# A gated delta-rule encoder: the query product of the scan taken from plain rows, its decay applied on the way out of the bank

## The chip, the cores and the metric

The kernel runs on one core of a Trainium2 chip, as one launch. The metric is the time of that launch on the device in microseconds (us); lower is better. The engines are called PE (matmul; PEld is its weight load), DVE (vector), ACT (scalar), POOL (GpSimd) and SP (which only issues DMAs here). ACT issues some DMAs too.

## The reference

Two layers; each has a mixer and a SwiGLU feed-forward network on 1040 rows (16 meta tokens and 1024 inputs) of width 1024. In the mixer, four heads of width 128 run a chunked gated delta rule in both directions of time. What matters here is how one direction makes its outputs (cut):

```python
def chunk_gated_delta_rule(q, k, v, g, beta):
    G = jnp.cumsum(g, axis=-1)                       # log-decay, <= 0, per head and row
    decay_mat = jnp.exp(jnp.where(incl, G[..., :, None] - G[..., None, :], -jnp.inf))
    ...
    attn = jnp.einsum('bnhid,bnhjd->bnhij', q, k) * decay_mat
    q_dec = q * jnp.exp(G)[..., None]
    ...
    def step(S, inp):
        u_c, w_c, qd_c, kd_c, a_c, gl_c = inp
        v_new = u_c - jnp.einsum('bhcd,bhde->bhce', w_c, S)
        o = jnp.einsum('bhcd,bhde->bhce', qd_c, S) + jnp.einsum('bhij,bhje->bhie', a_c, v_new)
        S = S * gl_c[..., None, None] + jnp.einsum('bhcd,bhce->bhde', kd_c, v_new)
        return S, o

o = (o_fwd + o_bwd)[:, N_PAD:]
o = o * lax.rsqrt(jnp.mean(o * o, axis=-1, keepdims=True) + RMS_EPS)
o = (o * dn_norm_w.astype(jnp.float32) * jax.nn.silu(zf)).reshape(Bsz, L, DN_WIDTH)
```

The factor `exp(G)` is one number for each row and head, so it can be put on the query before the product with the state `S`, or on the product's rows.

## The kernel before, in words

Everything is float32. The dense projections (`dense`, L157 to L159) split weights and activations into a high and a low part and add three products in one bank of the matmul's accumulator memory. ACT makes the high part of a weight tile (`whi`, L130), POOL, or DVE at places, the low part (`wlo`, L131). The delta rule's own products are plain float32.

A chunk is 128 rows; the kernel has nine (chunk 0 is the 16 meta rows). For one layer the order is: projections of k, q, v and of the gates; the decay matrices (`chunk_p`); the inverse of each chunk's triangular matrix, direction 0 and then 1 (`substitute` and `invert`, of which L545, L546, L581 and L582 are transposes and copies on DVE and L561 to L596 small matmuls with copies on ACT); the attention matrices and scaled queries (`chunk_a`); the scan; the output projection; the feed-forward network.

`chunk_a(c)` makes on PE the products of keys and queries of chunk `c` (`qk`, L490) into a bank of tag `b`, of which there are two. For each of two directions `d` ACT's queue loads a broadcast of `exp(G)` (`eg<-ged`, L494) and the decay matrix (`dt<-dtd`, L499), DVE multiplies the query with the first (L495) and `qk` with the second (L500), and SP stores both to DRAM (`aqd`, L497 and L502). `eg` and `dt` come from one ring of five buffers (`t2k`, tag `ck2`), so a load waits until the store out of the buffer five tiles earlier has landed. A bank of `qk` comes free with the second L500 of its chunk. Between these pieces PE works on dense projections; `jobs`, `jobs2` and `jobs3` are lists of such pieces, of which one of each is put behind every dense block of columns.

`scan_step(d, c)` runs one chunk of one direction with the state `St[d]` and two banks, `b0` and `b1` (tag `f` for direction 0, `b` for direction 1). Per head: `ks = K S` into `b0` (L806); DVE makes `r` (L809); `vr = Z r` into `b1` (L812); ACT reads `vr` scaled (L816) and plain (L818); `su` into `b0` (L822); the output `po` into `b1`: first the scaled query times `S` (L835), then the attention matrix times `vn` (L836), in one accumulation group; DVE updates the state (L844). The first direction to reach a chunk copies `po` out on ACT (L849) and stores it (`od`, L850); the second calls `finalize`, which loads it again (L862), adds (L863), normalises with ACT and DVE, transposes on PE (L875) and multiplies with the gate rows `sz` (L860, L876) into `O`. `rec` has four slots of 128x512 for each direction; V, K, A and the scaled query fill them.

The program's order on each engine is set when it is built, by a scheduler that goes by the priorities in the code (`at_prio`) and by its own estimate of times. An engine runs its instructions in that order, and so does each DMA queue.

## Time and profile before

| | |
|---|---|
| median of 3 runs | 2581.15 us (2574.96 to 2581.61) |
| the profiled execution's own time | 2581.81 us |
| its span (first to last instruction) | 2580.0 us |
| PE busy | 2501.8 us, 97% of the span |
| DVE, ACT, POOL busy | 64%, 41%, 44% |
| mean DMA rate | 140 GB/s, 360.04 MB in all |
| `chunk_a` and the inverse's second half run in | 225 to 300 us and 1515 to 1592 us |
| the scan runs in | 336 to 540 us and 1638 to 1842 us |

The profile lists instructions by line, engine and form with their durations, and for each idle time of an engine what ended it. Matmuls are pipelined, so one that is shown with 0.32 us can follow the last after 0.16 us; the distance of their starts is their cost. An idle time counts only where the engine that idles is the one that all others wait for, which is PE here.

### The profile page before, as it was taken

What the parts mean: (1) busy time and instruction counts of PE and PEld (TensorE: products, weight loads), DVE (VectorE), ACT (ScalarE), POOL (GpSimd) and SP (SyncE); (2) the same over time, 40 slices, a digit from 0 to 9 for tenths busy, and PEclk for the clock granted to TensorE, in tenths of its full rate; (3) what the DMA queues carried; (4) which work ended last, traced back from release to release, by engine and by line L of the source; (5) the groups of instructions that cost most, each with busy time, mean ns of one, the idle gap of its engine ahead of it and who ended that gap; (6) DMA issues with size and microseconds to landing.
All of it is one profiled execution on the core that took longest, in us unless ns stands there. A gap on an engine that the chain in (4) does not pass through costs nothing. (4 is left out here: it accounts for less than half of the span.)

```text
span 2580.0 us, 45319 instructions
## 1 busy us (share of the span) xinstructions
PE 2501.8 (97%) x17508; PEld 2284.7 (89%) x17508; DVE 1660.6 (64%) x2461; ACT 1045.1 (41%) x1945; POOL 1138.4 (44%) x869
## 2 busy tenths in 40 slices
PE   8999999999999999999999998999998999999998
PEld 6989899998899999999998987999977778887787
DVE  4678423648766666678656884235597776768664
ACT  5664232435233333444445742224452333334444
POOL 2141212325666666655420312212466676675663
PEclk9999999999999999999999999999999999999999
DMA  3445665524432222574323556556343322228631
GB/s 127 137 154 171 210 190 165 195 75 130 136 109 87 88 82 81 193 233 140 96 92 122 173 169 209 171 166 204 106 135 115 117 90 94 87 88 268 188 119 70
DMA packets 213764, 360.04 MB, mean 140 GB/s; under 512 B 25460, under 2 KB 87868, under 8 KB 213548
## 3 DMA queue, kind: packets, MB, share of 16 engines
q1 hardware_dynamic: 180300, 310.17, 36.6%
q10 hardware_dynamic: 31072, 42.61, 5.3%
q0 software_dynamic: 2176, 4.36, 0.5%
q8 instruction: 137, 2.24, 0.4%
q14 instruction: 79, 0.65, 0.1%
HBM read 266.60 MB, written 90.46 MB: 138 GB/s over the span
## 5 line engine op out<-in xcount | busy, mean ns | idle before, releaser
L131 POOL TENSOR_TENSOR wlo<-raw,whi 128x512 fp32r<-128x512 f32 x132 | 176.8, 1341 | 760.1 <-ACT whi L130 666.3
L157 PE MATMUL pacc<-a,whi 128*128 128x346 f32 (+1 forms) x808 | 263.9, 330 | 8.8 <-ACT whi L130 6.5
L159 PE MATMUL pacc<-a,wlo 128*128 128x346 f32 (+1 forms) x808 | 264.8, 329 | 0.5 <-DVE wlo L131 0.3
L157 PE MATMUL pacc<-b,whi 128*128 128x346 f32 (+2 forms) x672 | 235.4, 351 | 0.1
L159 PE MATMUL pacc<-b,wlo 128*128 128x346 f32 (+2 forms) x672 | 233.2, 348 | 0.2 <-POOL wlo L131 0.2
L158 PE MATMUL pacc<-a,whi 128*128 128x346 f32 (+1 forms) x688 | 227.1, 330 | 0.6 <-DVE a L178 0.3
L130 ACT ACTIVATE whi<-raw 128x512 fp32r<-128x512 f32 x168 | 105.2, 628 | 277.3 <-PE pacc L158 158.6
L158 PE MATMUL pacc<-b,whi 128*128 128x346 f32 (+2 forms) x580 | 200.9, 347 | 0.3 <-DVE b L906 0.3
L1048 POOL TENSOR_TENSOR wlo<-rw,whi 128x512 fp32r<-128x512 f32 x92 | 134.7, 1466 | 71.8 <-ACT whi L1047 70.4
L157 PEld LDWEIGHTS pacc<-a,whi 128*128 128x128 f32 x808 | 153.4, 191 | 13.2 <-ACT whi L130 8.2
L159 PEld LDWEIGHTS pacc<-a,wlo 128*128 128x128 f32 x808 | 154.2, 191 | 2.1 <-POOL wlo L131 0.5
L157 PEld LDWEIGHTS pacc<-b,whi 128*128 128x128 f32 x672 | 127.1, 189 | 12.0 <-issue 3.1
L158 PEld LDWEIGHTS pacc<-a,whi 128*128 128x128 f32 x688 | 131.4, 191 | 5.2 <-issue 3.3
L1048 POOL TENSOR_TENSOR a<-rw,a 128x512 fp32r<-128x512 f32 x64 | 105.5, 1651 | 68.3 <-ACT a L1047 68.2
L159 PEld LDWEIGHTS pacc<-b,wlo 128*128 128x128 f32 x672 | 127.3, 190 | 9.4 <-issue 0.8
L1048 POOL TENSOR_TENSOR b<-rw,b 128x512 fp32r<-128x512 f32 x64 | 92.4, 1446 | 84.2 <-ACT b L1047 50.1
L158 PEld LDWEIGHTS pacc<-b,whi 128*128 128x128 f32 x580 | 109.8, 189 | 7.5 <-DVE b L906 0.6
L1047 ACT ACTIVATE whi<-rw 128x512 fp32r<-128x512 f32 x92 | 57.8, 630 | 144.4 <-DVE rw L1293 82.5
L1294 DVE TENSOR_TENSOR rw<-raw,rw 128x512 f32<-128x512 f32 x44 | 98.9, 2247 | 1.2
L1289 DVE TENSOR_TENSOR rw<-rw,rw 128x512 f32<-128x512 f32 x44 | 68.2, 1550 | 48.2 <-POOL wlo L1048 30.9
L1048 POOL TENSOR_TENSOR wlo<-raw,whi 128x512 fp32r<-128x512 f32 x50 | 79.0, 1583 | 32.5 <-ACT whi L1047 32.2
L1047 ACT ACTIVATE b<-rw 128x512 fp32r<-128x512 f32 x64 | 40.3, 630 | 122.3 <-PE pacc L1066 35.2
(970 smaller groups left out, 8439.3 us busy)
## 6 DMA issues: line engine op xcount, KB each, us to landing
raw<-in_w_in SPq DMA_DIRECT2D x112, 256.0 KB
raw<-in_w_gu SPq DMA_DIRECT2D x104, 256.0 KB
rw<-in_w_gu SPq DMA_DIRECT2D x88, 256.0 KB
rw<-in_w_dn SPq DMA_DIRECT2D x94, 192.0 KB
rec<-aqd SPq DMA_DIRECT2D x62, 256.0 KB
rec<-vkd SPq DMA_DIRECT2D x61, 256.0 KB
raw<-in_w_out SPq DMA_DIRECT2D x48, 256.0 KB
b<-ad SPq DMA_DIRECT2D x45, 260.0 KB
```

What stands on the lines that cost most here:

```text
L130: whi_done[0] = act(out=hi, in_=raw[:, 0:kk, :], func=AF.Copy)
L131: (tt if lov[0] else ptt)(out=lo, in0=raw[:, 0:kk, :], in1=hi.bitcast(F32), op=ALU.subtract)
L157: mm(ps[:, :n], wh, xh[:, n0:n1], start=(k == 0), stop=False)
L158: mm(ps[:, :n], wh, xl[:, n0:n1], start=False, stop=False)
L159: mm(ps[:, :n], wl, xh[:, n0:n1], start=False, stop=(k == K - 1))
L1047: act(out=hi, in_=src, func=AF.Copy)
L1048: ptt(out=lo, in0=src, in1=hi.bitcast(F32), op=ALU.subtract)
L1289: tt(out=s1t, in0=A21, in1=A22, op=ALU.add)
L1294: tt(out=A21, in0=A11, in1=A21, op=ALU.subtract)
```

## The change

The scaled queries are no longer made. `gates` drops the table `ged`; `chunk_a` drops `eg`, L495 and the store of the scaled query, and `aqd` has half its size. `scan_step` multiplies the plain query rows `QT`, which stay in their place on chip, with the state into `b1` ahead of `vr` (L802 of the changed kernel), and ACT copies each head out into a new tile `qs` with the scale `negE`, which is minus `exp(G)` (L804). `po` then holds the attention part alone. The first direction to reach a chunk subtracts `qs` from `po` on DVE while it copies out; `finalize` lets POOL subtract `qs` from the loaded half (L857) before DVE adds. `O` becomes the tile of `QT` itself, and the gate rows `sz` come into the slot of `rec` that held the scaled query. The tiles `qs` take two of the ring's five buffers.

```diff
@@ -313,9 +313,8 @@
         szd = dram.tile([4, 128, L], F32, name=nm("szd"))
         yd = dram.tile([4, 128, L], F32, name=nm("yd"))
         vkd = dram.tile([9, 128, 2, 512], F32, name=nm("vkd"))
-        aqd = dram.tile([9, 2, 128, 2, 512], F32, name=nm("aqd"))
+        aqd = dram.tile([9, 2, 128, 512], F32, name=nm("aqd"))
         gd = dram.tile([72, 128], F32, name=nm("gd"))
-        ged = dram.tile([72, 128], F32, name=nm("ged"))
         rnd = dram.tile([8, L], F32, name=nm("rnd"))
         od = dram.tile([9, 128, 512], F32, name=nm("od"))
         hd = dram.tile([KT, 128, L], F32, name=nm("hd"))
@@ -393,9 +392,6 @@
             grows = gt[0:72, 2, 0:128]
             nc.vector.tensor_copy(grows, psT[0:72, 0:128])
             dma(gd, grows)
-            grows = gt[0:72, 2, 128:256]
-            act(out=grows, in_=psT[0:72, 0:128], func=AF.Exp, scale=-1.0)
-            dma(ged, grows)
             tt(out=fl(nGb), in0=fl(negG), in1=sv[0][:, 72:144], op=ALU.subtract)
             act(out=fl(negE), in_=psG[:, 0:72], func=AF.Exp)
             ts(out=fl(negE), in0=fl(negE), scalar1=-1.0, scalar2=None, op0=ALU.mult)
@@ -433,7 +429,6 @@
 
         at0 = [sb.tile([16, 4, 16], F32, tag=f"at0{d}", name=nm("at0")) for d in range(2)]
         P0 = [sb.tile([16, 4, 16], F32, tag=f"P0{d}", name=nm("P0")) for d in range(2)]
-        qd0 = sb.tile([128, 4, 16], F32, tag="qd0", name=nm("qd0"))
         dirs0 = [0] if last else [0, 1]
         dtd = dram.tile([9, 2, 128, 512], F32, name=nm("dtd"))
         Pd, Pv = [], []
@@ -489,17 +484,11 @@
             qk = bank("b").rearrange("p (h i) -> p h i", h=4)
             low(lambda: [mm(qk[0:n, h, 0:n], KTt[:, h, s0:s0 + n], QT[:, h, s0:s0 + n], start=True, stop=True) for h in range(H)])
             for d in (dirs0 if c == 0 else (0, 1)):
-                if c > 0 or d == 1:
-                    eg = t2k("eg")
-                    adma(eg[:, :, 0:n], ged[36 * d + 4 * c:36 * d + 4 * c + 4, 0:n].partition_broadcast(128))
-                    tt(out=qd0 if c == 0 else eg, in0=QT[:, :, s0:s0 + n], in1=eg[:, :, 0:n], op=ALU.mult)
-                    if c > 0:
-                        dma(aqd[c, d, :, 1, :], eg.rearrange("p a b -> p (a b)"))
                 dt_ = t2k("dt")
                 adma(dt_[0:n, :, 0:n], dtd[c, d].rearrange("p (h i) -> p h i", h=4)[0:n, :, 0:n])
                 tt(out=at0[d] if c == 0 else dt_, in0=qk[0:n, :, 0:n], in1=dt_[0:n, :, 0:n], op=ALU.mult)
                 if c > 0:
-                    dma(aqd[c, d, :, 0, :], dt_.rearrange("p a b -> p (a b)"))
+                    dma(aqd[c, d], dt_.rearrange("p a b -> p (a b)"))
 
 
         B = [slice(32 * b, 32 * b + 32) for b in range(4)]
@@ -764,8 +753,9 @@
 
         top = tc.cur_priority
         rec = sb.tile([128, 4 * L], F32, tag=Y[0][2], name=nm("rec"))
-        O = big(Y[0][1])
+        O = QT
         St = [t2k("S") for _ in range(2)]
+        qso = [t2k("qs") for _ in range(2)]
         vvs = [c4k("vv") for _ in range(2)]
         bk = [[bank("f"), bank("f")], [bank("b"), bank("b")]]
         fin = row(Y[1] + "f")
@@ -780,21 +770,17 @@
             n = 16 if c == 0 else 128
             s0 = 0 if c == 0 else 16 + 128 * (c - 1)
             base = d * 2048
-            V, K, A, Qd = (rec[:, base + 512 * i:base + 512 * i + 512].rearrange("p (h e) -> p h e", h=4) for i in range(4))
+            V, K, A, sz = (rec[:, base + 512 * i:base + 512 * i + 512].rearrange("p (h e) -> p h e", h=4) for i in range(4))
             dma(V[0:n].rearrange("p h e -> p (h e)"), vkd[c, 0:n, 0, :])
             if not final:
                 dma(K[0:n].rearrange("p h e -> p (h e)"), vkd[c, 0:n, 1, :])
             if c > 0:
-                dma(A.rearrange("p h e -> p (h e)"), aqd[c, d, :, 0, :])
-                if not first:
-                    dma(Qd.rearrange("p h e -> p (h e)"), aqd[c, d, :, 1, :])
+                dma(A.rearrange("p h e -> p (h e)"), aqd[c, d])
                 Zs = [Pv[d][:, (c - 1) * 4 + h, :] for h in range(4)]
                 As = [A[:, h, :] for h in range(4)]
-                Qs = [Qd[:, h, :] for h in range(4)]
             else:
                 Zs = [Z0[d][:, h, :] for h in range(4)]
                 As = [at0[d][:, h, :] for h in range(4)]
-                Qs = [qd0[:, h, :] for h in range(4)]
             b0, b1 = (v4(t) for t in bk[d])
             vv = vvs[d]
             vn, vs = v4(vv[:, 0:512]), v4(vv[:, 512:1024])
@@ -807,10 +793,18 @@
                 r = vn
                 for h in range(H):
                     stt(out=r[0:n, h, :], in0=ks[0:n, h, :], scalar=negE[0:n, d, c, h:h + 1], in1=V[0:n, h, :], op0=ALU.mult, op1=ALU.add)
+            need_o = not (c == 0 and d == 0)
+            qs = None
+            if need_o and not first:
+
+                qs = qso[d]
+                for h in range(H):
+                    mm(b1[0:n, h, :], QT[:, h, s0:s0 + n], St[d][:, h, :], start=True, stop=True)
+                for h in range(H):
+                    act(out=qs[0:n, h, :], in_=b1[0:n, h, :], func=AF.Copy, scale=negE[0:n, d, c, h:h + 1])
             vr = b1
             for h in range(H):
                 mm(vr[0:n, h, :], Zs[h], r[0:n, h, :], start=True, stop=True)
-            need_o = not (c == 0 and d == 0)
             for h in range(H):
                 if not final:
                     act(out=vs[0:n, h, :], in_=vr[0:n, h, :], func=AF.Copy, scale=bkd[0:n, d, c, h:h + 1])
@@ -831,9 +825,7 @@
             if need_o:
                 po = b1
                 for h in range(H):
-                    if not first:
-                        mm(po[0:n, h, :], Qs[h], St[d][:, h, :], start=True, stop=False, skip_group_check=True)
-                    mm(po[0:n, h, :], As[h], vn[0:n, h, :], start=first, stop=extra is None, skip_group_check=True)
+                    mm(po[0:n, h, :], As[h], vn[0:n, h, :], start=True, stop=extra is None, skip_group_check=True)
                     if extra is not None:
                         mm(po[0:n, h, :], at0[0][:, h, :], extra[0:n, h, :], start=False, stop=True, skip_group_check=True)
             if not final:
@@ -846,23 +838,26 @@
                 pof = po[0:n].rearrange("p h e -> p (h e)")
                 if c > 0 and c not in done:
                     done.add(c)
-                    act(out=vs.rearrange("p h e -> p (h e)"), in_=pof, func=AF.Copy)
+                    if first:
+                        act(out=vs.rearrange("p h e -> p (h e)"), in_=pof, func=AF.Copy)
+                    else:
+                        tt(out=vs, in0=po, in1=qs, op=ALU.subtract)
                     dma(od[c], vs.rearrange("p h e -> p (h e)"))
                 else:
-                    finalize(c, n, s0, po, pof)
-
-        def finalize(c, n, s0, po, pof):
+                    finalize(c, n, s0, pof, qs, sz[:, :, 0:n])
+
+        def finalize(c, n, s0, pof, qs, sz):
 
             ob = fin[:, 512 * (nfin[0] % 2):512 * (nfin[0] % 2) + 512]
             nfin[0] += 1
             o = ob[0:n].rearrange("p (h e) -> p h e", h=4)
-            sz = O[:, :, s0:s0 + n]
             dma(sz, szd[:, :, s0:s0 + n].rearrange("m p t -> p m t"))
             if c > 0:
                 dma(ob[0:n], od[c])
+                ptt(out=o, in0=o, in1=qs[0:n], op=ALU.subtract)
                 tt(out=ob[0:n], in0=pof, in1=ob[0:n], op=ALU.add)
             else:
-                nc.vector.tensor_copy(ob[0:n], pof)
+                tt(out=ob[0:n], in0=pof, in1=qs[0:n].rearrange("p h e -> p (h e)"), op=ALU.subtract)
             pt = v4(pa())
             st = sb.tile([128, 4], F32, tag="st", bufs=2, name=nm("st"))
             for h in range(H):
@@ -873,7 +868,7 @@
             tt(out=o, in0=o, in1=st[0:n].unsqueeze(2).to_broadcast([n, 4, 128]), op=ALU.mult)
             for h in range(H):
                 nc.tensor.transpose(pt[:, h, 0:n], o[:, h, :], ident[0:n, 0:n])
-            tt(out=sz, in0=pt[:, :, 0:n], in1=sz, op=ALU.mult)
+            tt(out=O[:, :, s0:s0 + n], in0=pt[:, :, 0:n], in1=sz, op=ALU.mult)
 
         nb = 8 if last else 9
         order = [(0, s) for s in range(4)]
```

Lines of the changed kernel from the scan on are 5 to 14 lower than before: L490 is L485 now, L500 is L489, L806 is L792, L812 is L807, L822 is L816, L836 is L828, L816 is L810, L863 is L858.

On DVE in layer 0, around the transposes of the second inverse, the kernel before has these rows (`pb` is the bank of `qk`, `b_357` a scratch row):

```order
L545 STREAM_TRANSPOSE b_357_3025<-x_1494 128x32x32
L495 TENSOR_TENSOR eg_2711<-b_38_169,eg_2711 128x512
L546 STREAM_TRANSPOSE x_1493<-x_1494 128x32x32
L296 TENSOR_TENSOR b_297_2620<-pacc_2727,rstd_81 128x346
L500 TENSOR_TENSOR dt_2715<-pb_2706,dt_2715 128x512
L581 COPY b_357_3025<-b_357_3025 32x16x32
L582 COPY b_357_3025<-b_357_3025 32x16x32
L581 COPY b_357_3025<-b_357_3025 32x16x32
L582 COPY b_357_3025<-b_357_3025 32x16x32
L495 TENSOR_TENSOR eg_2719<-b_38_169,eg_2719 128x512
L500 TENSOR_TENSOR dt_2723<-pb_2706,dt_2723 128x512
```

In the changed kernel the same place on DVE reads:

```order
L534 STREAM_TRANSPOSE b_338_2954<-x_1490 128x32x32
L535 STREAM_TRANSPOSE x_1489<-x_1490 128x32x32
L489 TENSOR_TENSOR dt_2680<-pb_2675,dt_2680 128x512
L489 TENSOR_TENSOR dt_2684<-pb_2675,dt_2684 128x512
L570 COPY b_338_2954<-b_338_2954 32x16x32
L571 COPY b_338_2954<-b_338_2954 32x16x32
L570 COPY b_338_2954<-b_338_2954 32x16x32
L571 COPY b_338_2954<-b_338_2954 32x16x32
L296 TENSOR_TENSOR b_290_2597<-pacc_2688,rstd_81 128x346
L489 TENSOR_TENSOR dt_2719<-pb_2714,dt_2719 128x512
```

The products with `eg` are gone, and both halves of a chunk (`dt_2680`, `dt_2684`) now stand ahead of the four copies, where before the second half stood behind them.

On PE in the scan of layer 0, one step of direction 0 reads before, from `su` on (`pf` are its two banks; L157 and L158 are dense work):

```order
L822 MATMUL pf_4323<-vv_4321,rec_4317 128x128 x4
L835 MATMUL pf_4324<-S_4319,rec_4317 128x128
L836 MATMUL pf_4324<-vv_4321,rec_4317 128x128
L835 MATMUL pf_4324<-S_4319,rec_4317 128x128
L836 MATMUL pf_4324<-vv_4321,rec_4317 128x128
L835 MATMUL pf_4324<-S_4319,rec_4317 128x128
L836 MATMUL pf_4324<-vv_4321,rec_4317 128x128
L835 MATMUL pf_4324<-S_4319,rec_4317 128x128
L836 MATMUL pf_4324<-vv_4321,rec_4317 128x128
```

In the changed kernel the query's four stand at the head of the step, behind `ks` (first piece), and the step's end has the attention's four alone (second piece; between the two pieces stand 28 dense rows, the four of `vr` and 22 dense rows):

```order
L157 MATMUL pacc_3820<-a_1_72,whi_3782 128x346
L792 MATMUL pf_4253<-S_4247,b_38_169 128x128 x4
L802 MATMUL pf_4254<-S_4247,b_37_168 128x128 x4
L158 MATMUL pacc_3820<-a_2_73,whi_3782 128x346
L159 MATMUL pacc_3820<-a_1_72,wlo_3783 128x346
```

```order
L816 MATMUL pf_4253<-vv_4251,rec_4246 128x128 x4
L157 MATMUL pacc_3889<-a_3_74,whi_3883 128x348
L828 MATMUL pf_4254<-vv_4251,rec_4246 128x128 x4
L158 MATMUL pacc_3889<-a_4_75,whi_3883 128x348
```

The query product moved from the end of the step to its head, and bank `pf_4254` is now written three times in a step (query, `vr`, output) instead of twice.

On ACT in the scan of layer 0, where both directions run, the changed kernel has:

```order
L804 ACTIVATE qs_4249<-pf_4254,negE_575 128x128 x4
L804 ACTIVATE qs_4250<-pb_4256,negE_575 128x128 x4
L810 ACTIVATE vv_4251<-pf_4254,bkd_577 128x128 x4
L812 ACTIVATE vv_4251<-pf_4254 128x512
L810 ACTIVATE vv_4252<-pb_4256,bkd_577 128x128 x4
L812 ACTIVATE vv_4252<-pb_4256 128x512
L130 ACTIVATE whi_3697<-raw_3699 128x512
```

Before, two steps at this stage read:

```order
L816 ACTIVATE vv_4322<-pb_4326,bkd_579 128x128 x4
L818 ACTIVATE vv_4322<-pb_4326 128x512
L816 ACTIVATE vv_4321<-pf_4324,bkd_579 128x128 x4
L818 ACTIVATE vv_4321<-pf_4324 128x512
L849 ACTIVATE vv_4322<-pb_4326 128x512
L849 ACTIVATE vv_4321<-pf_4324 128x512
```

Four scaled copies a step came in ahead of the reads of `vr`, and the copy of the output (L849) went to DVE.

## Prediction

> **What bounds the kernel now.** I read the page's busy times first, then the waits of PE over the whole span, then busy times by stage.
>
> ```profile
> PE 2501.8 (97%) x17508; PEld 2284.7 (89%) x17508; DVE 1660.6 (64%) x2461; ACT 1045.1 (41%) x1945; POOL 1138.4 (44%) x869
> ...
> PE pb L490 <- DVE dt L500: 7.5, 3, 3.7
> ...
> PE pb L561 <- DVE dt L500: 6.0, 2, 4.6
> ...
> 225.00:300.00 75.00, 69.93 (x613) 67.54 (x612) 56.81 (x102) 19.59 (x28) 16.84 (x11) 0.98 0.83 274
> 336.00:540.00 204.00, 202.69 (x1461) 196.91 (x1460) 94.19 (x227) 72.24 (x220) 52.84 (x39) 1.00 0.53 172
> 1515.00:1592.00 77.00, 68.30 (x634) 60.94 (x632) 54.78 (x96) 19.36 (x29) 16.79 (x11) 0.98 0.82 265
> 1638.00:1842.00 204.00, 203.69 (x1322) 187.72 (x1321) 90.26 (x209) 69.35 (x203) 49.94 (x40) 1.00 0.50 164
> ```
>
> The first row is the page's. The two rows with arrows give us in total, number and longest. In the stage rows stand the busy times of PE, PEld, DVE, ACT and POOL, then the granted clock, the DMA engines' share and GB/s. PE works 97% of the time, so the kernel gets faster only where PE idles or has less to do. The scan (rows 2 and 4) has next to no idle PE. The `chunk_a` stages (rows 1 and 3) have 5.1 and 8.7 us of it, at the highest DMA share, and their longest waits all end with L500, the product with the loaded `dt`. The timeline shows each of them and what follows:
>
> ```profile
> 269.65 1.13 PE L490 MATMUL pb<-b,b 128*128 128x128 f32 x8 [3.75 <-DVE dt L500]
> ...
> 270.97 0.49 PE L159 MATMUL pacc<-a,wlo 128*128 128x346 f32 x1
> 271.26 0.49 PE L157 MATMUL pacc<-a,whi 128*128 128x346 f32 x1
> ...
> 274.54 0.32 PE L157 MATMUL pacc<-a,whi 128*128 128x346 f32 x1
> 274.70 0.32 PE L158 MATMUL pacc<-a3f,whi 128*128 128x346 f32 x1
> ...
> 299.89 1.10 PE L561 MATMUL pb<-b,P 32*32 32x32 f32 x59 [1.33 <-DVE dt L500]
> ...
> 302.59 0.49 PE L157 MATMUL pacc<-a,whi 128*128 128x346 f32 x1
> ...
> 304.61 0.49 PE L158 MATMUL pacc<-a,whi 128*128 128x346 f32 x1
> ...
> 1559.32 1.13 PE L490 MATMUL pb<-a,a 128*128 128x128 f32 x8 [3.40 <-DVE dt L500]
> ...
> 1590.04 1.92 PE L561 MATMUL pb<-a,P 32*32 32x32 f32 x64 [4.65 <-DVE dt L500]
> ...
> 1592.91 0.63 PE L159 MATMUL pacc<-b,wlo 128*128 128x512 f32 x1
> 1593.34 0.63 PE L157 MATMUL pacc<-b,whi 128*128 128x512 f32 x1
> ...
> 1595.61 0.39 PE L157 MATMUL pacc<-b,whi 128*128 128x512 f32 x1
> 1595.84 0.39 PE L158 MATMUL pacc<-b,whi 128*128 128x512 f32 x1
> ```
>
> Starts, durations, and in brackets the idle time ahead. The four waits are 3.75 + 1.33 + 3.40 + 4.65 = 13.1 us. Behind three of them PE is slow for a while: starts lie 0.29 us apart at 271 and 0.16 us at 274.5; at 1593 it is 0.43 against 0.23. That costs 12 x 0.13 = 1.6 us after the first, 9 x 0.13 = 1.2 us from 302.6 to 304.9, and about 8 x 0.2 = 1.6 us plus some 0.7 us in L561's own block at 1590 (1.92 against a bit over 1.1): 5.1 us. So 18.2 us is what these waits cost, and all that this change can win.
>
> The Trainium skill (TensorE: Matmul & The Clock Gate, "What's actually happening") has the array at half clock after about one idle window of 3.4 us; the trace agrees at 269.65, and is harsher at 299.89, where an idle time of 1.33 us was enough.
>
> **Why L500 is late.** DVE's timeline and waits:
>
> ```profile
> 259.01 2.22 DVE L545 STREAM_TRANSPOSE b<-x 128x1024 f32<-128x1024 f32 x1
> ...
> 261.67 2.08 DVE L546 STREAM_TRANSPOSE x<-x 128x1024 f32<-128x1024 f32 x1
> ...
> 264.18 2.42 POOL L727 TENSOR_TENSOR b<-b,rstd 128x1040 f32<-128x1040 f32 x1 [5.47 <-DVE b L296]
> ...
> 264.73 2.16 DVE L581 COPY b<-b 32x512 f32<-32x512 f32 x1
> 266.90 0.42 DVE L582 COPY b<-b 32x512 f32<-32x512 f32 x1
> ...
> 268.82 0.68 DVE L500 TENSOR_TENSOR dt<-pb,dt 128x512 f32<-128x512 f32 x1
> ...
> DVE eg L495 <- DMA eg<-ged: 5.0, 4, 1.9
> ...
> DVE eg L495 <- DMA eg<-ged: 8.0, 6, 3.2
> ...
> 1585.82 0.93 DVE L495 TENSOR_TENSOR eg<-a,eg 128x512 f32<-128x512 f32 x1 [3.30 <-issue]
> ...
> 1589.20 0.69 DVE L500 TENSOR_TENSOR dt<-pb,dt 128x512 f32<-128x512 f32 x1
> ```
>
> L727 is a POOL product that ran beside the first copy. There are two causes. The L490 waits come when L500 stands behind two transposes and four copies. The L561 waits come from the ring of five buffers: DVE stands idle for an `eg` (5.0 us in the first stage, 8.0 in the second), since its load had to wait for a store.
>
> **The change, part by part.** For the rate of the ring and the pace of plain products there are these rows (a product is two records, x2, and the two rows start 0.22 us apart, the cost of one product):
>
> ```profile
> L495 DVE TENSOR_TENSOR eg<-b,eg x16: 652/691/1142, 232.6 to 297.5; 128x512 f32<-128x512 f32 x16
> ...
> eg<-ged ACTq DMA_DIRECT2D x16, 256.0 KB
> ...
> 367.91 0.38 PE L835 MATMUL pb<-S,rec 128*128 128x128 f32 x2
> 368.13 0.39 PE L836 MATMUL pb<-vv,rec 128*128 128x128 f32 x2
> ```
>
> *Removed in `chunk_a`.* 32 products L495 of 0.69 us and a small one, 22 us of DVE, and its waits for `eg`. Four transfers of 256 KB for each chunk and direction become two; of the 20 MB that the first stage moves in 75 us at 274 GB/s, 16 x 2 x 0.26 = 8.4 MB go. Two buffers of the ring are taken for a chunk instead of four. The 16 rows of L495 lie 64.9 / 15 = 4.3 us apart, 8.7 us a chunk; with half the tiles and the same time for a load and a store the ring can do one in 4.3 us. PE's new order in layer 0 asks for one in 24 dense rows and four of L485, 24 x 0.16 + 4 x 0.22 = 4.7 us. So the ring no longer limits, by a small margin, and the L561 waits go: 6.0 us and the 3.5 us of slow clock behind them. The DVE block at the transposes is now 2.22 + 2.08 + 2.16 + 3 x 0.42 + 4 x 0.69 = 10.5 us for two chunks, against 2 x 4.7 = 9.4 us of PE in layer 0, where the two banks cover the difference, and 13 and 15 dense rows of 0.23 us with 8 x 0.22, 8.2 us, in layer 1. There I leave a wait of 2.3 us and 1.6 us of slow clock behind it. Its bounds: nothing, or the whole 7.15 us of the L490 waits with their 1.6 us. Gain here: 18.2 - 3.9 = 14.3 us.
>
> *Removed elsewhere.* `ged`'s exponential and store, 30 loads of the scaled query in the scan: SP waits there for other things, so I count nothing; if SP were late, this would be a gain.
>
> *PE in the scan.* L835 is replaced by as many products of the same form (L802), so no PE time changes. They moved from the end of a step to its head.
>
> *ACT.* 31 steps get four scaled copies out of a bank; the nearest form is L816:
>
> ```profile
> L816 ACT ACTIVATE vv<-pf,bkd x64: 342/368/422, 346.8 to 1766.2; 128x128 f32<-128x128 f32 x56, 16x128 f32<-16x128 f32 x8
> ...
> L849 ACT ACTIVATE vv<-pf x10: 597/598/600, 373.5 to 1738.9; 128x512 f32<-128x512 f32 x10
> ...
> L863 DVE TENSOR_TENSOR b3f<-pb,b3f x5: 670/691/692, 441.9 to 520.4; 128x512 f32<-128x512 f32 x5
> ...
> L131 POOL TENSOR_TENSOR wlo<-raw,whi 128x512 fp32r<-128x512 f32 x25 | 32.6, 1302 | 170.7 <-ACT whi L130 155.4 <-PE pacc L159 15.2
> ```
>
> That is 31 x 4 x 0.368 = 46 us more on ACT, less 14 x 0.6 = 8.4 us of L849: from 72 to about 91 us of each 204. The new wait is `vr` (L807) on these copies, since both use `b1`; dense work queues behind L807 on PE. Between the query's products and L807 PE's order has 28 dense rows, 4.5 us, where one direction runs, and 9 to 12 dense and 8 plain rows, at least 3.8 us by row costs, where both do. The copies need 4 x 0.37 = 1.5 us, or 3.0 with the other direction's ahead. Before, `su` stood 3.0 to 3.5 us behind `vr` with the same four reads between, and PE did not wait. So I cost it at nothing; if the cover is gone, a step costs up to 1.5 us, 46 us in all.
>
> *DVE and POOL in the scan.* 14 subtractions of 0.69 us on DVE take L849's place; 16 on POOL of 1.30 us, 21 us, in `finalize`, off PE's path, with POOL busy 53 of 204 us. What waits behind them on POOL is `wlo` (L131), which POOL makes early. For the crowded place late in the scan, where PE's order is tight already, I add one wait of the size that stands there now:
>
> ```profile
> 507.11 0.63 PE L875 MATMUL pa<-ident,b3f 128*128 128x128 f32 x4 [0.88 <-DVE b3f L873]
> ```
>
> *SP.* Each of 17 loads of `sz` now waits until the last `finalize` of its direction has read the slot, and weight loads stand behind it; the scaled query's loads, 30 of them, waited like that before. I count nothing.
>
> **Sum.** The profiled execution took 2581.81 us, 0.7 us over the median of 2581.15. 2581.8 - 14.3 + 0.9 = 2568.4; 2568 us, by 0.5%. About 0.3% (7.7 us) is what a measurement of this kernel can tell from no change; the three runs shown spread over 0.26%.
>
> **The rivals.** (a) The L490 waits stay whole, as the DVE block still stands ahead of L489 and POOL stretches its copies (L581 took 2.16 us, its like 0.42). Then only the L561 part is won: 2581.8 - 9.5 + 0.9 = 2573 us. For it: the transposes and copies did not change. Against: L495 and its waits are gone from the block.
> (b) No change: what `chunk_a` wins is given back in the scan, since SP, held by an `sz` load, issues weights late. For it: SP already waits in the scan; against: the waits it replaces are of one kind. 14 us in 17 loads, 0.8 us each, would do: 2582 us.
> (c) Slower: the scaled copies are late. ACT runs in order, and where an `L130` (0.63 us) or a wait for the other direction's bank stands ahead, L807 waits. At 0.8 us a step, 31 x 0.8 = 25 us, so 2568 + 25 = 2593 us; from 0.7 us a step (21 us over 31 steps) the kernel is slower by over 0.3%.
> (d) Slower: POOL's 16 subtractions block DVE in the scan for their length, each on the path: 2568 + 21 = 2589 us. The trace has DVE copies stretched by 1.7 us at 264.73, and the products around them not. The Trainium skill (SBUF — State Buffer, "Who interferes with whom") has an exclusive lock between DVE and POOL, which this would be.
>
> **How the numbers follow.** The forecast has 0.55, by itself 2562 to 2575 us; (a) 0.17, (b) 0.13, (c) 0.11, (d) 0.04. The range: from 2559 (all 18.2 us, with the runs' spread) to 2584, which takes in (a) and (b) and leaves out (c) and (d). Faster by over 0.3% (below 2573.4): nearly all of the forecast and half of (a), 0.61. Within 0.3%: the rest of both, and (b), 0.24. Slower: (c) and (d), 0.15.
>
> **What would show it.** In the changed profile PE's waits on `dt` (L485, L550 behind L489) should sum to 0 to 4 us instead of 13.5, the DMA share of the stage stay at or below 0.8, the half-clock stretches there shrink to one or none, and PE show no wait of L807 on ACT `qs`. The prediction is wrong if L807 waits on L804 in most steps, if L485 still waits over 3 us in both layers, or if waits on `whi` or `wlo` appear in the scan.

## The result: 11 us faster, and the profile after

The changed kernel takes 2565.38 us in the median (2561.09 to 2566.29, 7 runs), the kernel before 2576.26 us beside it (2568.55 to 2581.61, 7 runs): 0.995 of it, 95% interval 0.9937 to 0.9963, which is 9.5 to 16 us. The prediction was 2568 us from a profiled 2581.8 us, 0.9948 of it. The profiled execution took 2561.09 us (span 2558.7), one of its quickest; that of before was among its slowest. Their 21 us of difference are therefore more than the change is worth, and the stages have to be compared one by one.

Engines over the span, from the page of the changed kernel (the row of before stands in the prediction):

```profile
PE 2494.0 (97%) x17508; PEld 2280.6 (89%) x17508; DVE 1641.7 (64%) x2442; ACT 1070.0 (42%) x2053; POOL 1157.3 (45%) x885
```

Busy time by stage, before. The four stretches are, for layer 0 and then layer 1: from the first product of `chunk_a` to the first of the scan, and from there to the first product of the feed-forward network (the scan with `w_out` behind it). Columns as before; the first number behind the stretch is its length.

```profile
166.40:340.60 174.20, 168.73 (x1764) 162.07 (x1764) 115.05 (x225) 63.56 (x92) 33.11 (x31) 0.98 0.54 177
340.60:613.20 272.60, 269.91 (x1976) 263.58 (x1974) 138.13 (x302) 99.97 (x267) 81.89 (x60) 1.00 0.48 155
1508.60:1640.30 131.70, 123.00 (x1282) 109.25 (x1282) 64.99 (x114) 39.95 (x61) 31.55 (x22) 0.97 0.65 210
1640.30:1892.80 252.50, 250.68 (x1706) 233.84 (x1704) 130.16 (x274) 95.50 (x247) 74.19 (x57) 1.00 0.49 160
```

The same four of the changed kernel, and then the two windows of `chunk_a` that the prediction showed of before:

```profile
162.60:326.70 164.10, 163.67 (x1759) 158.20 (x1759) 101.12 (x208) 62.95 (x90) 32.59 (x31) 1.00 0.40 132
326.70:602.60 275.90, 271.94 (x1981) 265.89 (x1980) 144.13 (x309) 113.49 (x324) 92.60 (x68) 0.99 0.45 142
1494.50:1614.60 120.10, 120.00 (x1282) 107.22 (x1282) 52.65 (x98) 39.91 (x61) 30.86 (x22) 1.00 0.43 144
1614.60:1872.20 257.60, 252.59 (x1706) 235.22 (x1704) 133.91 (x281) 108.09 (x300) 84.50 (x65) 0.99 0.46 150
...
225.00:300.00 75.00, 75.00 (x837) 72.63 (x836) 39.89 (x75) 25.28 (x37) 19.97 (x14) 1.00 0.52 171
...
1505.00:1582.00 77.00, 76.90 (x754) 68.07 (x753) 39.63 (x72) 24.03 (x35) 19.77 (x14) 1.00 0.52 172
```

`chunk_a` went from 174.2 + 131.7 to 164.1 + 120.1 us, 21.7 less: PE has no idle time left there, the clock is full, and the DMA share fell from 0.83 to 0.52. The scan went from 272.6 + 252.5 to 275.9 + 257.6 us, 8.4 more: PE's idle time (length less busy) grew from 4.5 to 9.0 us and its busy time by 3.9 us for nearly the same instructions, of which 3.4 us are two stretches of 3.4 us at half the granted clock, behind the waits shown next. The other 8 us of the 21 lie in stages that the change hardly touches, and are scatter: from the first transpose of `k_out` to `chunk_a` the profiles have 57.2 us before and 54.5 after, but 54.2 in a kernel with the gates of before (e2 below) and 59.6 in one with the gates as changed (e7).

The waits of PE that are new in the scan, from the list over the whole span (total, number, longest); no row on `dt` is left in it:

```profile
PE pacc L157 <- ACT b L900: 1.8, 1, 1.8
...
PE pacc L157 <- ACT a L900: 1.3, 1, 1.3
...
PE pacc L158 <- DVE a L901: 0.9, 2, 0.7
```

L900 and L901 split the rows `yd` for the dense products of `w_out`, which fill PE late in the scan. The timeline shows how layer 1 gets there:

```profile
1759.44 1.30 POOL L857 TENSOR_TENSOR a3f<-a3f,qs 128x512 f32<-128x512 f32 x1 [3.29 <-DMA a3f<-od]
...
1760.70 2.95 POOL L131 TENSOR_TENSOR wlo<-raw,whi 128x512 fp32r<-128x512 f32 x2
...
1760.77 1.75 DVE L1284 TENSOR_TENSOR rw<-rw,rw 128x512 f32<-128x512 f32 x1 [3.30 <-POOL a3f L857]
1762.44 1.22 DVE L865 SCALAR_TENSOR_TENSOR st<-st,g 128x4 f32<-128x4 f32 x1
...
1763.69 0.20 ACT L866 ACTIVATE st<-st 128x4 f32<-128x4 f32 x1 [2.34 <-DVE st L865]
1763.81 1.13 ACT L900 ACTIVATE b<-a 128x512 fp32r<-128x512 f32 x2
...
1764.47 0.50 PE L157 MATMUL pacc<-b,whi 128*128 128x512 f32 x1 [1.77 <-ACT b L900]
...
1766.53 0.63 PE L159 MATMUL pacc<-b,wlo 128*128 128x512 f32 x1
```

POOL's subtraction waits for `od`. L1284, the first sum of the next stage's weights, stands in DVE's queue and waits for that subtraction: its tile `rw` is of the ring of five buffers, of which the two `qs` now hold two until POOL has read them. (Before, this sum ran at 360.3 and 1656.4 us, early in the scan; now at 469.9 and 1760.8.) Behind it stands L865, behind that ACT's L866, behind that in ACT's queue L900, and PE idles 1.77 us and then runs at half clock (0.63 us for a row of 0.40). A second delay lies in the same chain: beside POOL's two L131, L1284 and L865 took 1.75 and 1.22 us, against 0.69 and 0.15 us where they ran alone. In layer 0, where L1284 was done by 472 us, its stop does not explain the waits of 1.26 and 0.67 us at 499 and 500 us.

### The profile page after: what moved, and what is told of

Same layout as the page of the kernel before. It is cut to its first block, busy times and chain, and to the rows that moved or that the text cites. A ratio compares the mean times of both kernels' runs of the same rounds, so it can differ in the third digit from the quotient of the medians.

```text
span 2558.7 us, 45283 instructions
## 1 busy us (share of the span) xinstructions
PE 2494.0 (97%) x17508; PEld 2280.6 (89%) x17508; DVE 1641.7 (64%) x2442; ACT 1070.0 (42%) x2053; POOL 1157.3 (45%) x885
## 5 line engine op out<-in xcount | busy, mean ns | idle before, releaser
L131 POOL TENSOR_TENSOR wlo<-raw,whi 128x512 fp32r<-128x512 f32 x132 | 175.1, 1329 | 638.0 <-ACT whi L130 523.8
L157 PE MATMUL pacc<-a,whi 128*128 128x346 f32 (+1 forms) x808 | 264.1, 330 | 9.3 <-ACT whi L130 6.4
L157 PE MATMUL pacc<-b,whi 128*128 128x346 f32 (+2 forms) x672 | 233.9, 349 | 1.8 <-ACT b L900 1.8
L158 PE MATMUL pacc<-a,whi 128*128 128x346 f32 (+1 forms) x688 | 225.8, 328 | 0.9 <-DVE a L901 0.9
L158 PE MATMUL pacc<-b,whi 128*128 128x346 f32 (+2 forms) x580 | 200.4, 346 | 0.0
L157 PEld LDWEIGHTS pacc<-a,whi 128*128 128x128 f32 x808 | 152.8, 190 | 13.8 <-ACT whi L130 7.9
L157 PEld LDWEIGHTS pacc<-b,whi 128*128 128x128 f32 x672 | 126.8, 189 | 13.6 <-issue 3.1
L158 PEld LDWEIGHTS pacc<-a,whi 128*128 128x128 f32 x688 | 130.4, 190 | 5.4 <-issue 2.9
L158 PEld LDWEIGHTS pacc<-b,whi 128*128 128x128 f32 x580 | 109.5, 189 | 6.9 <-issue 0.4
L1284 DVE TENSOR_TENSOR rw<-rw,rw 128x512 f32<-128x512 f32 x44 | 69.9, 1589 | 46.9 <-POOL wlo L1043 30.9
```

Source lines behind the costliest of these rows:

```text
L131: (tt if lov[0] else ptt)(out=lo, in0=raw[:, 0:kk, :], in1=hi.bitcast(F32), op=ALU.subtract)
L157: mm(ps[:, :n], wh, xh[:, n0:n1], start=(k == 0), stop=False)
L158: mm(ps[:, :n], wh, xl[:, n0:n1], start=False, stop=False)
L1284: tt(out=s1t, in0=A21, in1=A22, op=ALU.add)
```

## The experiments

Ratios are to the kernel before on the same chip, with their 95% intervals; 0.001 is 2.6 us.

**Ahead of the scan: what brought the waits on `dt`**

**e2: the scan half alone.** `chunk_a`, the gates and their buffers as before, the scan as changed:

```
 aqd = dram.tile([9, 2, 128, 2, 512], F32, ...)
+eg = t2k("eg")
+adma(eg[:, :, 0:n], ged[...].partition_broadcast(128))
+tt(out=qd0 if c == 0 else eg, in0=QT[...], in1=eg[:, :, 0:n], op=ALU.mult)
+if c > 0: dma(aqd[c, d, :, 1, :], eg...)
```

> Only the scan half of the change: chunk_a and the gates still load the decay rows, make the scaled queries on VectorE and store them, as before the change, but the scan does not read them and uses plain rows as changed. Theory A: the wins ahead of the scan are gone and the scan's cost stays, so 5 to 9 us above the kernel before's 2576, 2581 to 2585 us, with the waits of PE on dt back at 13 us in all. Rival B (the scan half is free): 2575 to 2577 us. In either case the distance to the changed kernel is what the chunk_a half is worth by itself: 16 to 20 us by A, 11 by B.

Measured: 1.0026 (1.0015 to 1.0036), 6.7 us slower than before. PE's waits on `dt` are back:

```profile
PE pb L561 <- DVE dt L500: 7.7, 2, 5.6
PE pb L490 <- DVE dt L500: 3.1, 3, 2.0
```

Theory A holds: the scan half costs about 7 us, and the `chunk_a` half is worth 1.0026 - 0.995 = 0.0076, 19.6 us (17.8 us by the changed kernel's second value, 0.9957 in e3). In this profile `chunk_a` takes 169.7 + 130.6 us, 16.1 more than as changed.

**e6: the moves alone.** e2 without its products on DVE:

```
-tt(out=qd0 if c == 0 else eg, in0=QT[:, :, s0:s0 + n], in1=eg[:, :, 0:n], op=ALU.mult)
```

> As the kernel with the scan half alone, but the 32 products with the query (L495 of the kernel before) are left out: the decay rows are loaded into the ring and stored again as they are, so that the ring of five buffers and the transfers stay as before the change and VectorE's work is that of the changed kernel. Theory A (the waits of the second kind, L561 before, came from the ring and its transfers; those of the first kind, L490 before, from VectorE's block of transposes, copies and products): only the second kind stays, 6.0 us and 3.5 us of slow clock, so 2565 + 9.5, 2573 to 2577 us. Rival B (VectorE's work was behind all four waits): 2565 to 2567 us. Rival C (the transfers were behind all four): 2579 to 2584 us.

Measured: 1.0005 (0.9996 to 1.0015), 14 us above the changed kernel's 0.995. Its `chunk_a` windows and waits:

```profile
163.70:333.70 170.00, 166.83 (x1758) 159.80 (x1758) 100.75 (x208) 63.36 (x91) 32.73 (x31) 0.99 0.52 177
1506.80:1634.50 127.70, 122.97 (x1283) 109.53 (x1283) 52.49 (x98) 40.20 (x61) 31.11 (x22) 0.97 0.62 201
```

```profile
PE pb L490 <- DVE dt L499: 4.5, 2, 3.8
PE pb L568 <- DVE dt L499: 1.9, 1, 1.9
```

297.7 us against 284.2 of the changed kernel, with DVE as busy as there (100.8 and 101.1, 52.5 and 52.7). The theory fell: waits of the first kind came with the moves and with no work of DVE.

**e7: the products alone.** The changed kernel with 32 products put back on DVE, and nothing loaded or stored:

```
+eg = t2k("eg")
+tt(out=eg[:, :, 0:n], in0=QT[...], in1=QT[...], op=ALU.mult)
```

> The changed kernel with 32 products of the same size as those removed put back on VectorE in chunk_a (query by query, into a buffer of the ring that nobody reads), without the loads and stores of the decay rows. Theory A: the waits of the first kind (7.15 us and 1.6 us of slow clock) come back, those of the second don't: 2565 + 8.7, 2571 to 2576 us. Rival B (VectorE's work was behind all four waits): 2579 to 2584 us. Rival C (the transfers were): 2565 to 2567 us.

Measured: 0.9971 (0.996 to 0.9982). That is 1.4 to 2.1 thousandths, 4 to 5 us, above the changed kernel's two values, less than the two intervals can tell. The stage says more: DVE is 11 us busier in each, and PE waits for no `dt`. Its one wait on DVE there, in layer 0, ends with another product (L723):

```profile
PE pacc L157 <- DVE b L723: 1.5, 1, 1.5
...
168.20:333.70 165.50, 164.03 (x1758) 158.10 (x1758) 112.61 (x225) 61.88 (x89) 34.63 (x31) 1.00 0.39 130
1505.20:1625.20 120.00, 120.00 (x1283) 107.36 (x1283) 64.00 (x114) 40.31 (x61) 33.87 (x22) 1.00 0.43 143
```

So 285.5 us, 1.3 more than as changed. DVE's block of transposes, copies and products alone did not make the waits on `dt`.

**e13: the ring as before, with small moves.** e2 without products, and 512 bytes in each of the 32 loads and stores:

```
 eg = t2k("eg")
+adma(eg[0:1, 0, 0:n], ged[36 * d + 4 * c:36 * d + 4 * c + 1, 0:n])
+dma(aqd[c, d, 0:1, 1, 0:n], eg[0:1, 0, 0:n])
```

> The reverse: a buffer of the ring is taken for each chunk and direction, loaded and stored on the same queues as before the change, but with 512 bytes in place of 256 KB, and no product on VectorE. Theory A (the ring): the waits on dt stay, since load and store hold the buffer for their latency of some 2 to 3 us whatever their size: 8 to 13 us, 0.999 to 1.002 of the kernel before. Rival B (the bytes): no such waits, 0.995 to 0.997. Between the two values, both have a share.

Measured: 0.9965 (0.9951 to 0.9978).

```profile
165.40:329.70 164.30, 163.93 (x1758) 158.32 (x1758) 99.80 (x208) 62.92 (x91) 33.35 (x31) 1.00 0.41 132
1498.70:1618.50 119.80, 119.80 (x1282) 107.42 (x1282) 52.27 (x98) 40.11 (x61) 31.80 (x22) 1.00 0.43 144
```

284.1 us, as changed. The same buffers, issues and queues cost nothing when the moves are small; e6 differs in their size alone and takes 13.6 us more.

**e12: the same bytes, past the ring.** The decay rows copied from DRAM to DRAM:

```
+if c > 0: adma(aqd[c, d, :, 1, :]..., ged[...].partition_broadcast(128))
```

> The changed kernel with the scan as changed, but in chunk_a the decay rows are copied from DRAM to DRAM, 256 KB read and 256 KB written for each chunk and direction as before the change, past the ring of five buffers and with no product on VectorE. It tells apart what is left of the chunk_a half, since the products alone brought no wait back and the moves alone brought nearly all. Theory A (the ring: a load waits for a buffer that a store still reads): no waits of PE on dt, 0.995 to 0.997 of the kernel before. Rival B (the transfers themselves: the DMA engines, 0.83 busy there before, are late with dt): the waits stay, 8 to 13 us in all, 0.999 to 1.002.

Measured: 1.0007 (0.9996 to 1.0018). By the numbers this is rival B, but not by its mechanism: the copies, which wait for no buffer, were issued earlier, around `k_out` (first row; the last but one number is the DMA share), and the window of `chunk_a` (second row) has a share of 0.52 and 1.5 us of idle PE. Its middle third (third row) has a share of 0.86, and PE's one wait on `dt` in the whole profile, 0.9 us, lies there:

```profile
100.00:125.00 25.00, 21.07 (x132) 19.38 (x131) 13.89 (x18) 11.18 (x19) 2.17 (x4) 1.00 1.00 323
225.00:300.00 75.00, 73.52 (x819) 70.29 (x818) 46.98 (x85) 29.02 (x44) 18.03 (x12) 0.98 0.52 172
...
250.00:275.00 25.00, 24.06 (x185) 23.40 (x185) 19.96 (x32) 7.78 (x11) 6.99 (x5) 1.00 0.86 280
```

The loss is scattered. The span is 15.9 us longer than the changed kernel's; 4.8 of them lie between `k_out` and the scans of the two layers, and 6.6 between layer 0's first feed-forward product and layer 1's `k_out`, which the edit does not touch. A high share without the ring brought almost no wait on `dt`, which speaks against the share alone; but the copies ran at another time than those of e6. Whether in `chunk_a` the full-size moves delay `dt` in the DMA engines or by holding buffers longer stays open.

**In the scan: what its 8 us are**

**e3: the changed kernel again**, as the mark for e4, e8 and e9.

> The changed kernel again, unaltered, beside the other three on one chip and as the mark for them. All theories: 0.995 of the kernel before, within 0.0015. PE's waits on L900 and L901 at the end of the scan are expected in the same places, about 1.9 us in layer 0 and 1.7 us in layer 1, with a half-clock stretch of 3.4 us behind the first of them; the waits of PE at the transposes of k_out, which differed between the profiles (3.8 us here, 3.1 and 5.2 with the gates of before), are expected to differ again.

Measured: 0.9957 (0.9942 to 0.9972); waits of 1.26 and 0.70 us on L900 and L901 in layer 0 and of 1.61 us in layer 1.

**e1: the scan without the additions.** No scaled copies, no subtractions; the decay of the query is left out:

```
-mm(b1..., QT..., St...); act(out=qs..., scale=negE...)
+mm(po[0:n, h, :], QT[:, h, s0:s0 + n], St[d][:, h, :], start=True, stop=False)
-tt(out=vs, in0=po, in1=qs, op=ALU.subtract)
+act(out=vs..., in_=pof, func=AF.Copy)
-ptt(out=o, in0=o, in1=qs[0:n], op=ALU.subtract)
```

> The changed kernel with the scan's additions taken out: the plain query's products go straight into the output's bank as the scaled ones did before, with no scaled copies on ScalarE, no subtractions on VectorE and GpSimd (the decay of the query is left out). Everything ahead of the scan stays as changed. Theory A (the change wins about 18 to 21 us ahead of the scan and gives 5 to 9 us of it back in the scan, by waits on the splitting of the output rows, L900): 5 to 9 us below the changed kernel's 2565, that is 2556 to 2560 us, with the PE waits on L900 gone and no half-clock stretch at 502 and 1765 us. Rival B (the scan's additions are free, as the prediction's +0.9 us had it, and the rest is scatter between executions): 2564 to 2566 us.

Measured: 0.9942 (0.9927 to 0.9956), 2 to 4 us below the changed kernel's two values: less than A's 5 to 9, and by the intervals not told from B. The scans' 275.0 + 252.4 us are 6.1 less than as changed, PE has no wait of more than 0.4 us on the splitting and no half clock there.

**e4: the subtraction of `finalize` on DVE.**

```
-ptt(out=o, in0=o, in1=qs[0:n], op=ALU.subtract)
+tt(out=o, in0=o, in1=qs[0:n], op=ALU.subtract)
```

> The changed kernel with the subtraction of finalize (L857) on VectorE instead of GpSimd. Theory A: the scaled copies hold two of the five buffers of the ring until their last read, so the first sum of the next stage's weights (L1284) waits in VectorE's queue for GpSimd's subtraction (3.30 us at 1757.5), the chain of finalize stands behind it, ScalarE's L866 waits for that and L900 stands behind L866; with the last read on VectorE itself nothing waits there: layer 1's 1.77 us and 1.7 us of slow clock go, 2 to 4 us below the changed kernel; layer 0 as it was. Rival B (GpSimd's 16 subtractions block VectorE by sharing its port): 4 us or more below. Rival C (VectorE gets 16 x 0.69 = 11 us more in the crowded place): 0 to 3 us above.

Measured: 0.9926 (0.9913 to 0.994), 2552.12 us: 8 us below the changed kernel on the same chip, and the quickest of all. Windows of the scans:

```profile
328.00:598.10 270.10, 269.06 (x1981) 264.25 (x1981) 140.02 (x317) 113.49 (x324) 80.64 (x60) 1.00 0.44 145
1612.60:1865.70 253.10, 250.81 (x1706) 233.83 (x1704) 136.55 (x289) 108.29 (x300) 74.61 (x57) 1.00 0.46 153
```

523.2 us, 1.9 less than before the change, with all of ACT's copies in it. At the place shown above DVE now runs

```profile
1758.03 0.69 DVE L857 TENSOR_TENSOR a3f<-a3f,qs 128x512 f32<-128x512 f32 x1 [2.11 <-DMA a3f<-od]
1758.75 0.69 DVE L1284 TENSOR_TENSOR rw<-rw,rw 128x512 f32<-128x512 f32 x1
1759.36 0.68 DVE L858 TENSOR_TENSOR a3f<-pf,a3f 128x512 f32<-128x512 f32 x1
...
1762.00 1.14 ACT L900 ACTIVATE b<-a 128x512 fp32r<-128x512 f32 x2
```

L1284 waits for nothing, and L900 starts with no idle time of ACT ahead of it. The gain is twice what theory A had, since layer 0's waits went as well: there ACT's queue, as changed, has L866 of a `finalize` ahead of the second piece of L900, and in e4 behind it. The order differs in layer 1 too. Counted from the scan's first product L900 starts no earlier (149.4 us against 149.2), but PE has other small products to do meanwhile: `vr` of direction 1 stands at 142.4 us of the scan instead of 146.1. By its size the gain is in rival B's range as well. B alone cannot give 8 us: in the changed kernel's profile the DVE instructions that overlap one of the 16 subtractions are longer by 3.0 us in all. How much the free buffer, the shorter chain of `finalize`, the free POOL and the other order gave is not separated.

**e8: an earlier edge for L900** in layer 0:

```
-read.get((1, 1)) if j and not last else None
+read.get((1, 2)) if j and not last else None
```

> The changed kernel with one edge moved: in layer 0 the splitting of the output rows' second and third piece (L900) may start after the backward step of chunk 2 instead of chunk 1. Theory A (in layer 0 the dense work that fills the scan's end runs out because L900 is let go too late for the longer step): the 1.26 and 0.67 us on L900 and L901 and 1.7 us of slow clock go, 2 to 4 us below the changed kernel. Rival B (the fill is used up earlier and the last steps stand bare): the same idle time appears later in the scan, 0 to 3 us above. Layer 1 as it was in both.

Measured: 0.9945 (0.9932 to 0.9958). Layer 0's waits on L900 and L901 are gone and its scan takes 271.8 us, 4 less than as changed; layer 1 keeps its 1.6 us. A holds by the trace; by the ratio, 3 us, within both intervals.

**e9: the sum of the weights after the scan.**

```
+read["end"] = tt(out=O[:, :, s0:s0 + n], ...)
+after(tt(out=s1t, in0=A21, in1=A22, op=ALU.add), read.get("end") if f == 0 else None)
```

> The changed kernel with the first sum of the next stage's weights (L1284) made to follow the last product of the scan (L871) on VectorE. Theory A: VectorE no longer stands at L1284 for the ring's buffer in the middle of the crowded end; layer 1's wait of 1.77 us on L900 goes with its 1.7 us of slow clock, 2 to 4 us below the changed kernel; layer 0 keeps its waits. Rival B (ScalarE's 46 us of scaled copies are what makes L900 late): no change, the wait stays at 1.5 to 1.8 us. If the sum is then too late for the stage that needs it, a new wait shows at the head of that stage, and the gain is lost.

Measured: 0.9967 (0.9954 to 0.998). Layer 1's wait on L900 is gone as A has it: POOL still subtracts and the steps stand where they stood, but L900 starts 146.7 us behind the scan's first product instead of 149.2. So L1284's place in DVE's queue made that wait. Taking the wait away won no time here: 0.74 us on L901 stay, and a new wait stands where `w_out` takes the scan's output, larger than the one that went (one of 2.44 us stands there in layer 0):

```profile
1869.45 0.55 PE L157 MATMUL pf<-o,whi 128*128 128x256 f32 x1 [2.96 <-DVE b L905]
```

**e14: e4 and e8 together.**

> The subtraction on VectorE and the earlier edge for L900 together. Theory A (both took away the same waits at the end of the scan in layer 0, of which the first left none): as with the subtraction alone, 0.9926 within 0.0015. Rival B (the gains add up): 0.9915 or less.

Measured: 0.9928 (0.9916 to 0.9941), as e4 alone: both take away the same waits.

**e15: the scaled copies twice**, on e4:

```
+for _ in range(2):
     for h in range(H): act(out=qs[0:n, h, :], in_=b1[0:n, h, :], func=AF.Copy, scale=negE...)
```

> The subtraction on VectorE as in e4_subtract_dve, with each of the four scaled copies of a step made twice on ScalarE, 46 us more in the two scans together per layer pair (31 steps x 4 x 0.37). It measures how near the prediction's rival of late copies was. Theory A (28 dense rows, or 12 dense and 8 plain ones, cover 1.5 us of copies with room): most steps cover 3 us as well; 0 to 10 us above e4's 0.9926, that is 0.9926 to 0.996. Rival B (ScalarE is at its limit): 0.75 to 1.5 us a step, 23 to 46 us, 1.002 to 1.010, with PE waiting at L807.

Measured: 1.0045 (1.003 to 1.0059), 0.0119 above e4: 31 us, as much as 1.0 us for each of 31 steps. In the profiles the two scans take 25.8 us more.

```profile
326.90:612.30 285.40, 275.79 (x1982) 269.10 (x1980) 144.91 (x317) 129.96 (x388) 80.90 (x60) 0.98 0.41 137
1624.00:1887.60 263.60, 253.38 (x1707) 234.39 (x1705) 143.63 (x290) 124.55 (x363) 74.57 (x57) 1.00 0.44 146
```

The waits of PE from 325 to 545 us:

```profile
PE pb L802 <- DVE b3f L859: 3.1, 1, 3.1
PE pb L808 <- ACT qs L805: 2.8, 2, 2.4
PE pb L817 <- ACT vv L811: 2.0, 2, 1.1
```

This is rival B's number and not its sign: PE waits for `qs` (L807, here L808) twice, not in most steps. Up to 488 us PE has no wait of over 0.3 us. Those that there are lie at the ends of the scans: 8.7 us between 488 and 510 us with 13.7 us of half clock, and 9.3 us between 1765 and 1888 us. The steps stand further apart (`vr` of the last step of direction 0 in layer 0 comes 147.7 us behind the scan's first product, against 136.5 in e4), and dense work covers that until it runs out.

## Why the prediction was right, and where its steps were not

*`chunk_a`, gain 14.3 us.* The signs that it named for its being right came: no wait on `dt`, a DMA share of 0.52, no wait of L807 on `qs`. But its gain was too small on both terms. The 3.9 us left in layer 1 were not there: no wait on `dt` remains in either layer. And the slow clock behind the old waits was taken from row distances as 5.1 us, while the granted clock was halved for 3.4, 3.4 and 6.8 us there; PE still idled in the first 1.6 us of the last, so 12.0 us of work ran at half speed, up to 6.0 us lost. The stages gave 21.7 us in the profiles; by e2, 17.8 to 19.6.

*Why L500 was late.* This step failed, though its sum did not rest on it alone. The prediction had the L490 waits come from DVE's block and the L561 waits from the ring. The products alone bring neither (e7, 1.3 us), the ring with small moves brings neither (e13, 0), and the full-size moves alone bring 13.5 us (e6), of which the larger waits stand at L490. Its working of the ring's rate, 4.3 against 4.7 us, therefore described nothing that bound. What bound was the size of the moves, at a DMA share of 0.83; by which way is open (e12).

*ACT's copies at nothing.* Right: with them in, e4's scan is not longer than before, and the changed kernel's profile has no wait of PE on them. Their size was put too high, at 1.5 us a step and 46 us in all; four overlap on ACT and take 1.12 us, and ACT's busy time rose by 25 us net:

```profile
494.67 1.12 ACT L804 ACTIVATE qs<-pb,negE 128x128 f32<-128x128 f32 x4
```

Doubled, they cost 31 us (e15), and not as rival (c) had it, by waits at L807, but at the ends of the scans.

*DVE and POOL in the scan, +0.9 us.* The mis-sized term: 8.4 us in the profiles, 6.7 by e2. One wait of 0.88 us was allowed for the crowded end; the trace has 1.26, 0.67 and 1.77 us on L900 and L901, small ones around them, and half clock behind both places. "Off PE's path" was the step that failed. In layer 1 the subtraction on POOL is the last reader of `qs`, `qs` holds two buffers of the ring, and DVE's queue stops at the next taker (e9 shows it for the wait of 1.77 us). In layer 0 the edge that lets L900 start came too late for the longer step (e8); why the step is longer there, no run takes apart. The prediction asked what waits behind L857 on POOL, and not who takes the buffers that it reads from.

*Rivals.* (a) did not come: no L490 wait stayed. (b) came in part: the scan gave back 7 to 8 of 20 us, by another way than SP. (d) has the right instruction and a wrong size: its 16 subtractions stretched DVE by 3.0 us in all, summed over the DVE instructions that overlapped one against the lower quartile of the same line and form, and not by 21.

The two misses, 4 to 7 us too little gain and 6 to 8 us too little loss, cancelled. That the time came out right is luck; its parts were not right.

## What to carry to other kernels

When data is kept on chip instead of sent through DRAM, ask which ring the new tile comes from, who reads it last, and what in an in-order queue waits for the buffer it holds; put that last read on the engine whose queue would otherwise stop. Where a stage waits on a loaded tile at a DMA share of 0.8, test bytes, instructions and buffers apart; here it was the bytes. A busy share of 40% does not say how much slack a helper has: double its work once, and look where the waits appear.

## What the runs showed of the hardware

PE's clock can halve behind short waits, and then for 3.4 us or a multiple of it (6.8 us at 1588 us before the change). Behind 1.26 and 0.67 us at 500, and behind 1.77 us at 1764 us, the granted clock was one half for 3.4 us. It need not: of the eight profiles with a wait of 1.5 to 1.8 us on L900 in layer 1, four have such a stretch behind it (waits of 1.53, 1.60, 1.66 and 1.77 us) and four have none (1.57, 1.59, 1.61 and 1.66 us), and behind the 3.40 us at 1559.32 before the change the clock stayed full. The Trainium skill (TensorE: Matmul & The Clock Gate, "What's actually happening") gives 3.4 us as the window that the clock is decided by, which agrees with the length; its condition of about one idle window is not what these traces show.

DVE and POOL, side by side, can hold each other up until an instruction ends. L865, four elements in each partition, takes 0.15 us on DVE, and beside POOL's subtraction it took 1.28 us and ended as that did:

```profile
477.97 1.28 DVE L865 SCALAR_TENSOR_TENSOR st<-st,g 128x4 f32<-128x4 f32 x1
...
477.03 2.21 POOL L857 TENSOR_TENSOR b3f<-b3f,qs 128x512 f32<-128x512 f32 x1 [2.99 <-DMA b3f<-od]
```

POOL's instruction was long itself (1.30 us elsewhere) beside DVE's L310 ahead of this one (476.76 to 478.05 us). The Trainium skill (SBUF — State Buffer, "Who interferes with whom") has a pair of ports shared by the two as an exclusive lock, where the order of issue decides who waits; these two rows agree.
